# fp32 value halves, a later second rotation and another queue for B and C in a state-space stage

## The chip, the cores and the metric

The kernel runs on one core of a Trainium2 chip. The metric is the device time of one execution, in microseconds (us): 2155.58 us as the median of 3 runs of the kernel before (2154.86 to 2159.57). The profile is of one further execution, which took 2159.01 us and whose first to last instruction span 2157.2 us; 1.8 us lie around the span.

## The reference

A trunk of two layers over 256 frames of width 2048, all in fp32. Layer 0 mixes with a state-space model, layer 1 with latent attention; each is followed by a gated MLP with a causal convolution. The change touches the mixer of layer 0 alone:

```python
def s5_mixer(u, ...):                       # u: (1, 256, 2048), 128 groups of 16 channels
    # per group: a complex diagonal state of size 64, decayed by ab_re + i*ab_im at each frame
    x_re = einsum('blgp,gnp->blgn', ub, bb_re)          # and x_im
    hs_re, hs_im = scan over the frames
    y = einsum('blgn,gpn->blgp', hs_re, c_re) - einsum('blgn,gpn->blgp', hs_im, c_im) + d_skip * ub
    y = jax.nn.gelu(y)
    val, gate = jnp.split(y @ w_glu + b_glu, 2, axis=-1)   # w_glu: (2048, 4096)
    return val * sigmoid(gate)
```

The last two lines are the linear unit ("GLU"): its value half is the first 2048 columns of `w_glu`, its gate half the other 2048.

## The kernel before

**Precision.** A weight that is multiplied on the matmul engine (TensorE, PE) is loaded as fp32 into a `raw` buffer, and split there: ScalarE (ACT) writes the part `whi` that the fast one-pass type fp32r holds, VectorE (DVE) writes the rest, `wlo`. The activations are split in the same way. `mm3` (L107 to L110) makes one product of three fp32r matmuls: high by high, high by low, low by high.

**The state-space stage** (function `s5`) treats the 128 groups in 16 blocks of 8 groups. The loop over `n` runs 18 times and is a software pipeline: iteration `n` has `part_k` and `part_e` of block `n`; `part_v`, `part_r` (first rotation and the scan along the frames) and `part_h` (second rotation, of the scanned state) of block `n-1`; and `part_c` (the output) of block `n-2`. `lead_e` and `lead_f` make the operands of later blocks: products of powers of the decay with the matrices B and C (DVE, L442), two of which are added by a DMA that GpSimd (POOL) issues. `part_k` sends a matrix `K` to memory (`kd`, by ACT's queue) and reads it back in Toeplitz order (`TP`, by SyncE's queue, SP). SP also loads B and C (`bc`) and all weights.

Every fourth block a quarter of the 2048 channels is done: `part_d` applies the gelu, turns the result and writes it, split, to the activation tiles. From then on the part of the GLU that needs only this quarter's rows of `w_glu` can run. It is cut into *units*: `glu_early(f, n, b, half)` takes the rows of quarter `b`, 512 columns of the value (`half` 0) or the gate (`half` 1), 1 MB of weights, 2 splits on ACT and 2 on DVE, and 24 matmuls of 512 columns; then `glu_keep` copies or adds both results to an accumulator in SBUF. Columns 0 to 1023 of both halves are done in this way, four units to a quarter. One unit is traced at the end of an iteration where one is left. The list is worked off by a generator (`glu_steps`), and the iteration in which a generator is found to be exhausted brings no unit: quarter 0 is finished in iteration 5 and has its units in iterations 5 to 8, quarter 1 in 10 to 13, quarter 2 in 15 to 17. What is left, one unit of quarter 2 and four of quarter 3, comes first in `glu_rest`, before the 16 units of the remaining columns.

**Order.** The kernel is written for a planner which gives each engine a list in the order of the trace where the operands are there by its own costs, and lets a later instruction pass where they aren't. Each engine then works its list in order. So the matmuls of a unit lie among those of the next block. The planner also gives out the buffers of a tag: `raw` has 2, `whi` and `wlo` 3 each; the normalised input `X` occupies both `raw` buffers until `scale_x` of the last quarter.

Of the kernel before, what the change touches and what calls it, by code (L numbers as in the profile page):

```python
# [8 lines left out]
F32 = mybir.dt.float32  # L9
# [6 lines left out]
P = 128  # L16
# [28 lines left out]
def tile_trunk(ctx: ExitStack, tc: tile.TileContext, a: dict):  # L45
# [19 lines left out]
    def accb():  # L65
        return T(ps, [P, 512], F32, "acc")
# [172 lines left out]
    def glu_load(n, b, half, slots=(None, None)):  # L239
        col = half * D + n * 512  # L240
        return wunit(glu_w[b][:, :, col : col + 512], 4, 512, slots=slots)

    def glu_mm(bank, b, tb, halves):
        hk, u = halves
        for i, (wh, wl) in enumerate(u):
            for k in range(hk):
                j = i * hk + k
                mm3(bank, *acts(tb, 4 * b + j), wh[:, k, :], wl[:, k, :], b == 0 and j == 0, b == 3 and j == 3)

    def glu_early(f, n, b, half):  # L250
        hv = glu_load(n, b, half)
        banks = [accb(), accb()]
        for tb in range(NB):
            hk, u = hv
            for i, (wh, wl) in enumerate(u):
                for k in range(hk):
                    j = i * hk + k
                    mm3(banks[tb], *acts(tb, 4 * b + j), wh[:, k, :], wl[:, k, :], j == 0, j == 3)
        glu_keep(f, n, b, half, banks)
# [11 lines left out]
    def s5(f):  # L271
        with tc.tile_pool(name="s5", bufs=2) as q1, tc.tile_pool(name="dr", bufs=2, space=bass.MemoryType.DRAM) as dr:
# [7 lines left out]
            for k in range(8):  # L280
                sync.dma_start(X[k // 4][:, k % 4, :], a["xs"][k])
            gX = T(q1, [P, 512], F32, "gX", 1)
            dB = T(q1, [P, 512], F32, "dB", 1)
# [154 lines left out]
            def product(tag, bufs, sb, i):  # L438
# [4 lines left out]
                return o  # L443

            def lead_e(n):
                if n >= nb:
                    return
                if n % PB == 0:
                    zs[n // PB] = powers(n // PB)
                bc[n] = T(q1, [P, 4, NP, 16], F32, "bc", 3)  # L450
                sync.dma_start(bc[n], a["sBC"][n])
                E[n], e2 = product("e1", 3, n, 0), product("e2", 2, n, 1)
                pool.dma_start(E[n], e2, accum_op=ALU.add)
# [104 lines left out]
            def glu_steps(b):  # L558
                for n in range(2):
                    for half in range(2):  # L560
                        yield glu_early(f, n, b, half)

            def part_d(qt, yg):
                act_tiles()
                act.activation(yg, yg, AF.Gelu_apprx_tanh)
                for hh in range(2):
                    ptv = wk().rearrange("p (t m) -> p t m", t=4)
# [6 lines left out]
                    for tb in range(NB):  # L574
                        hi, lo = acts4(tb, qt, slice(0, 4))
                        src = ptv.rearrange("p t (j c) -> p t j c", j=4)[:, :, :, 16 * tb : 16 * tb + 16]
                        split(av(hi), av(lo), src)

            todo, zs, bc, E, F, fr, U, TP, ET, H = [], {}, {}, {}, {}, {}, {}, {}, {}, {}
            nb = 4 * PB  # L580

            rs = first_norm()
            lead_e(0)
            lead_f(0)
            scale_x(rs, 0)
            for n in range(nb + 2):
# [9 lines left out]
                if n < nb:  # L596
                    U[n], TP[n] = part_k(n, F[n], bc.pop(n))
                    ET[n] = part_e(E.pop(n))
                if 0 <= n - 1 < nb:
                    H[n - 1] = part_h(n - 1, R, *fr.pop(n - 1))  # L600
                if n >= 2 and m % PB == PB - 1:
                    part_d(m // PB, yg)
                    todo.append(glu_steps(m // PB))
                if n == 0:
                    lead_e(1)
                lead_f(n + 1)
                lead_e(n + 2)
                if n < 3:
                    scale_x(rs, n + 1)
                if todo and next(todo[0], True) is True:  # L610
                    todo.pop(0)
        return todo
# [588 lines left out]
```

## Time and profile before

| | |
|---|---|
| median of 3 runs | 2155.58 us (2154.86 to 2159.57) |
| profiled execution | 2159.01 us, span 2157.2 us |
| PE busy | 2057.1 us, 95% of the span |
| DVE busy | 1377.6 us, 64% |
| ACT busy | 1092.6 us, 51% |
| granted PE clock, mean of the span | 0.992 |

PE's busy time is modelled: each matmul counts to the end of its pipeline, so that the share of a stretch can be near 100% while more matmuls would fit. Instructions carry the line of the kernel; where a helper issues them (`split` is L73 on ACT and L74 on DVE, `mm3` L108 to L110, `tiled` L419), it is the helper's line, and the tiles' names tell what they are. An engine's idle time is put down to what ended it. PEld are the weight loads of PE, SPq and ACTq the instructions by which SP and ACT issue DMAs.

### The profile page before, as it was taken

The page shows a single profiled execution, that of the slowest core. Times are in us where ns is not written, and L with a number is a line of the kernel's source. Part 1 is how long each engine was busy: PE and PEld are TensorE (multiplying, and loading weights), DVE is VectorE, ACT ScalarE, POOL GpSimd, SP SyncE. Part 2 cuts the span into 40 slices and gives each one's busy share as a digit, 9 for nine tenths or more (in the row PEclk, how much of TensorE's full clock was granted, in tenths as well). Part 3 has the DMA queues.
Part 4 walks back from the last instruction along what each step waited for, and adds up shares of the span by engine and source line. Part 5 has one row for each costly group of instructions (what it writes and reads, how often), then busy time and mean ns, then how long its engine had stood idle before and what let it go on. Part 6 is the DMA issues. An engine that isn't in the chain of part 4 may idle for free.

```text
span 2157.2 us, 30703 instructions
## 1 busy us (share of the span) xinstructions
PE 2057.1 (95%) x12372; PEld 1754.2 (81%) x12372; DVE 1377.6 (64%) x1931; ACT 1092.6 (51%) x1669; POOL 32.2 (1%) x73
## 2 busy tenths in 40 slices
PE   3798998999999999999999999999999999999998
PEld 2566777888888888888878998788888888888886
DVE  8898766665466556656685665566546655665567
ACT  5565445554455445534474554655545544553444
POOL 1000000000000000000000000000000000000000
PEclk9899999999999999999999999999999999999999
DMA  5676766455555556555554334545556555555654
GB/s 148 188 197 175 236 195 190 159 195 176 196 194 187 184 195 193 180 193 194 190 193 138 123 126 152 197 156 191 180 193 197 183 187 196 189 182 189 201 184 149
DMA packets 291967, 392.15 MB, mean 182 GB/s; under 512 B 10224, under 2 KB 205424, under 8 KB 291056
## 3 DMA queue, kind: packets, MB, share of 16 engines
q1 hardware_dynamic: 287216, 377.86, 53.8%
q0 software_dynamic: 2304, 8.39, 2.2%
q10 hardware_dynamic: 2304, 3.93, 0.5%
q8 instruction: 97, 1.59, 0.3%
q14 instruction: 46, 0.38, 0.1%
HBM read 375.73 MB, written 6.03 MB: 177 GB/s over the span
## 4 chain that ended last, share of the span: by engine, by line
PE 82%; DMA 7%; DVE 6%; ACT 3%; issue 1%; SPq 0%; POOL 0%; DVEq 0%; POOLq 0%; ACTq 0%
PE wk L723 28%; PE wk L725 15%; PE acc L109 10%; PE acc L110 9%; PE acc L108 9%; DMA raw<-in_w_glu 3%; PE wk L109 2%; PE wk L110 2%; PE wk L108 2%; DVE wlo L74 1%; PE wk L419 1%; ACT whi L73 1%; DVE x L74 1%; ACT junk L135 1%; DMA kd<-K 1%
## 5 line engine op out<-in xcount | busy, mean ns | idle before, releaser
L74 DVE TENSOR_TENSOR wlo<-raw,whi 128x1024 fp32r<-128x1024 f32 (+1 forms) x636 | 755.8, 1191 | 603.5 <-ACT whi L73 597.7
L73 ACT ACTIVATE whi<-raw 128x1024 fp32r<-128x1024 f32 (+1 forms) x636 | 654.2, 1032 | 758.4 <-PE wk L723 310.5
L723 PE MATMUL wk<-act,whi 128*128 128x512 f32 x2688 | 673.6, 392 | 0.0
L723 PEld LDWEIGHTS wk<-act,whi 128*128 128x128 f32 x2688 | 483.8, 189 | 86.9
L725 PEld LDWEIGHTS wk<-act,wlo 128*128 128x128 f32 x2688 | 366.7, 190 | 26.2
L725 PE MATMUL wk<-act,wlo 128*128 128x256 f32 x2688 | 374.8, 282 | 0.0
L110 PE MATMUL acc<-whi,hl 128*128 128x512 f32 x652 | 255.9, 394 | 0.0
L109 PE MATMUL acc<-wlo,hh 128*128 128x512 f32 x652 | 255.6, 392 | 0.0
L108 PE MATMUL acc<-whi,hh 128*128 128x512 f32 x652 | 253.3, 388 | 0.0
L109 PEld LDWEIGHTS acc<-wlo,hh 128*128 128x128 f32 x652 | 122.4, 188 | 28.2
L108 PEld LDWEIGHTS acc<-whi,hh 128*128 128x128 f32 x652 | 122.4, 188 | 27.4 <-ACT hh L73 0.5
L110 PEld LDWEIGHTS acc<-whi,hl 128*128 128x128 f32 x652 | 122.6, 188 | 24.5
L108 PE MATMUL acc<-whi,act 128*128 128x512 f32 (+1 forms) x316 | 119.9, 383 | 7.2 <-ACT whi L73 4.3
L109 PE MATMUL acc<-wlo,act 128*128 128x512 f32 (+1 forms) x316 | 121.4, 385 | 2.8 <-DVE wlo L74 2.7
L110 PE MATMUL acc<-whi,act 128*128 128x512 f32 (+1 forms) x316 | 119.1, 377 | 0.4 <-DVE act L74 0.4
L782 DVE SCALAR_TENSOR_TENSOR cv<-gs,cw,cv 128x255 f32<-128x255 f32 (+1 forms) x168 | 81.0, 482 | 17.2 <-ACT cv L780 14.3
L108 PEld LDWEIGHTS acc<-whi,act 128*128 128x128 f32 x316 | 59.7, 190 | 20.1 <-ACT whi L73 5.3
L109 PEld LDWEIGHTS acc<-wlo,act 128*128 128x128 f32 x316 | 60.2, 191 | 16.8 <-DVE wlo L74 5.7
L780 ACT ACTIVATE cv<-gs,cb,cw 128x256 f32<-128x256 f32 x84 | 49.9, 594 | 45.8 <-DVE gs L731 45.8
L110 PEld LDWEIGHTS acc<-whi,act 128*128 128x128 f32 x316 | 60.1, 190 | 11.1 <-DVE act L74 0.9
L74 DVE TENSOR_TENSOR x<-raw,x 128x1024 fp32r<-128x1024 f32 x36 | 43.2, 1221 | 32.7 <-ACT x L73 32.7
L108 PE MATMUL acc<-x,act 128*128 128x512 f32 (+1 forms) x164 | 56.6, 347 | 7.1 <-DVE act L197 3.6
(277 smaller groups left out, 2243.3 us busy)
## 6 DMA issues: line engine op xcount, KB each, us to landing
raw<-in_w_gate SPq DMA_DIRECT2D x88, 1024.0 KB
raw<-in_w_up SPq DMA_DIRECT2D x88, 1024.0 KB
raw<-in_w_down SPq DMA_DIRECT2D x88, 1024.0 KB
raw<-in_w_glu SPq DMA_DIRECT2D x32, 1024.0 KB
raw<-in_w_o SPq DMA_DIRECT2D x16, 1024.0 KB
e<-e POOLq DMA_DIRECT2D x16, 512.0 KB, 6.1
TP<-kd SPq DMA_DIRECT2D x64, 128.0 KB
raw<-in_w_ukv SPq DMA_DIRECT2D x8, 1024.0 KB
```

The source lines that it names most:

```text
L73: act.activation(hi, src, AF.Copy)
L74: (eng or dve).tensor_tensor(lo, src, hi.bitcast(F32), op=ALU.subtract)
L108: pe.matmul(o, lh, rh, start=first, stop=False)
L109: pe.matmul(o, lh, rl, start=False, stop=False)
L110: pe.matmul(o, ll, rh, start=False, stop=last)
L135: act.activation(junk[:, :w], src, AF.Square, accum_out=stat)
L419: pe.matmul(o[32 * j : 32 * j + 32, g * P : (g + 1) * P], lhs(g, j), rhs(g, j), start=g == 0 and i == 0, stop=diag is None and g == NG - 1 ...
L723: pe.matmul(o, w, pair(kt), start=kt == 0, stop=False)
L725: pe.matmul(o[:, 0, :], w, pair(kt)[:, 0], start=False, stop=kt == KT - 1)
L780: act.activation(cv[:, ft, :], gv[:, ft, :], AF.Identity, scale=cw[:, 2, n : n + 1], bias=cb[:, n : n + 1])
L782: dve.scalar_tensor_tensor(cv[:, ft, sh:], gv[:, ft, : S - sh], cw[:, 2 - sh, n : n + 1], cv[:, ft, sh:], op0=ALU.mult, op1=ALU.add,)
```

## The change

1. **Value halves in fp32.** For quarters 0 to 2, the units of the value half multiply plain fp32 tiles: `part_d` keeps an unsplit copy `plain` of the quarter (4 more copies on ACT), the weights are loaded, as two DMAs of 512 KB, into one buffer each of `whi` and `wlo` instead of `raw`, they aren't split, and a unit has 8 fp32 matmuls in place of 24 fp32r ones. Gate halves, and all of quarter 3, stay as they were.
2. **Units in three steps.** A unit is now traced in three pieces (load and first 128 frames; last 128 frames; `glu_keep`). The first lies between `part_e` and `part_h`, so that the matmul of the second rotation is traced behind it, the others at the end of the iteration. `advance` goes on to the next quarter's generator when one is exhausted: an iteration has one unit from iteration 5 to 17, and quarters 0, 1 and 2 are done in iterations 5 to 16. `part_d` stands before `part_h` now.
3. **B and C.** `bc` is loaded three blocks ahead by ACT's queue, right behind `part_k`, instead of two blocks ahead by SP's (the first three still by SP).
4. `scale_x` of the last quarter is done in iteration 1 instead of 2, and `gX` shares the buffer of `yg`.

```diff
+    plain = {}
+
     def glu_early(f, n, b, half):
-        hv = glu_load(n, b, half)
         banks = [accb(), accb()]
+        if half == 0 and b in plain:
+            raws = [T(env["wp"], [P, 2, 512], F32, t, env["wb"]) for t in ("whi", "wlo")]
+            for i, raw in enumerate(raws):
+                sync.dma_start(raw, glu_w[b][:, 2 * i : 2 * i + 2, n * 512 : (n + 1) * 512])
+        else:
+            hk, u = glu_load(n, b, half)
         for tb in range(NB):
-            hk, u = hv
-            for i, (wh, wl) in enumerate(u):
-                ...
+            if half == 0 and b in plain:
+                for j in range(4):
+                    pe.matmul(
+                        banks[tb], plain[b][:, j, tb * P : (tb + 1) * P], raws[j // 2][:, j % 2, :],
+                        start=j == 0, stop=j == 3,
+                    )
+            else:
+                ...
+            yield
         glu_keep(f, n, b, half, banks)
...
-            gX = T(q1, [P, 512], F32, "gX", 1)
+            gX = T(q1, [P, 512], F32, "yg", 1)
...
+            def fetch(n, eng):
+                if n < nb:
+                    bc[n] = T(q1, [P, 4, NP, 16], F32, "bc", 3)
+                    eng.dma_start(bc[n], a["sBC"][n])
+
             def lead_e(n):
...
-                bc[n] = T(q1, [P, 4, NP, 16], F32, "bc", 3)
-                sync.dma_start(bc[n], a["sBC"][n])
...
-                        yield glu_early(f, n, b, half)
+                        yield from glu_early(f, n, b, half)
+                        yield
...
                 act.activation(yg, yg, AF.Gelu_apprx_tanh)
+                if qt < 3:
+                    plain[qt] = T(q1, [P, 4, S], F32, "plain", 1)
...
                         split(av(hi), av(lo), src)
+                        if qt < 3:
+                            act.activation(av(plain[qt][:, :, tb * P : (tb + 1) * P]), src, AF.Copy)
...
+            def advance():
+                while todo and next(todo[0], True) is True:
+                    todo.pop(0)
+
             rs = first_norm()
+            for n in range(3):
+                fetch(n, sync)
...
                     U[n], TP[n] = part_k(n, F[n], bc.pop(n))
+                    fetch(n + 3, act)
                     ET[n] = part_e(E.pop(n))
-                if 0 <= n - 1 < nb:
-                    H[n - 1] = part_h(n - 1, R, *fr.pop(n - 1))
                 if n >= 2 and m % PB == PB - 1:
                     part_d(m // PB, yg)
                     todo.append(glu_steps(m // PB))
+                advance()
+                if 0 <= n - 1 < nb:
+                    H[n - 1] = part_h(n - 1, R, *fr.pop(n - 1))
                 if n == 0:
                     lead_e(1)
                 lead_f(n + 1)
                 lead_e(n + 2)
-                if n < 3:
+                if n < 2:
                     scale_x(rs, n + 1)
-                if todo and next(todo[0], True) is True:
-                    todo.pop(0)
+                if n == 1:
+                    scale_x(rs, 3)
+                advance()
+                advance()
```

More of the change, by code (lines that the diff above doesn't have):

```diff
@@ L248, in glu_mm @@
                 mm3(bank, *acts(tb, 4 * b + j), wh[:, k, :], wl[:, k, :], b == 0 and j == 0, b == 3 and j == 3)
+    plain = {}
     def glu_early(f, n, b, half):
-        hv = glu_load(n, b, half)
         banks = [accb(), accb()]
-        for tb in range(NB):
-            hk, u = hv
-            for i, (wh, wl) in enumerate(u):
-                for k in range(hk):
-                    j = i * hk + k
-                    mm3(banks[tb], *acts(tb, 4 * b + j), wh[:, k, :], wl[:, k, :], j == 0, j == 3)
+        if half == 0 and b in plain:
[4 more added lines that the diff above has]
+            hk, u = glu_load(n, b, half)
+        for tb in range(NB):
+            if half == 0 and b in plain:
[5 more added lines that the diff above has]
+            else:
+                for i, (wh, wl) in enumerate(u):
+                    for k in range(hk):
+                        j = i * hk + k
+                        mm3(banks[tb], *acts(tb, 4 * b + j), wh[:, k, :], wl[:, k, :], j == 0, j == 3)
+            yield
         glu_keep(f, n, b, half, banks)
```

## The prediction

> **What bounds the kernel now.** I read the page first. PE is busy for 95% of the span, so outside the stage that is changed the matmuls set the time, and nothing there is touched. The question is what one stage is worth.
>
> ```profile
> span 2157.2 us, 30703 instructions
> PE 2057.1 (95%) x12372; PEld 1754.2 (81%) x12372; DVE 1377.6 (64%) x1931; ACT 1092.6 (51%) x1669; POOL 32.2 (1%) x73
> ```
>
> Next, the timeline of PE for the places of the loop. Below stand `part_k` of block 5 (iteration 5), the first matmul of the first GLU unit, and `part_k` of block 15.
>
> ```profile
> 82.78 0.67 PE L419 MATMUL wk<-f,bc 128*32 128x128 f32 x16
> ...
> 90.19 0.51 PE L108 MATMUL acc<-whi,act 128*128 128x512 f32 x1
> ...
> 215.96 1.08 PE L419 MATMUL wk<-f,bc 128*32 128x128 f32 x32
> ```
>
> I call 80 to 216 us the stretch: ten iterations, 5 to 14. Then the busy time by stretches (each engine: busy us and instructions; then PE clock, DMA share, GB/s):
>
> ```profile
> 100.00:120.00 20.00, 19.57 (x276) 15.55 (x274) 20.00 (x37) 12.46 (x28) 1.06 (x4) 1.00 0.65 193
> 80.00:216.00 136.00, 118.20 (x1498) 91.07 (x1493) 121.78 (x195) 79.17 (x153) 8.99 (x14) 0.95 0.67 180
> 216.00:240.00 24.00, 23.84 (x246) 19.54 (x246) 15.39 (x25) 13.35 (x21) 0.00 (x0) 1.00 0.62 193
> 240.00:300.00 60.00, 54.39 (x228) 41.64 (x227) 42.09 (x55) 27.41 (x35) 0.00 (x0) 1.00 0.78 237
> ```
>
> The third figure of a row is PE, the fifth DVE. In the stretch DVE is busy for 121.8 of 136 us (89.5%), and from 100 to 120 without a pause: DVE is the first limit there. PE has 17.8 us without a matmul. From 216 on PE takes over. DVE's groups in the stretch show what it does:
>
> ```profile
> L442 DVE TENSOR_TENSOR f<-zs,bc 128x1024 f32<-128x1024 f32 x20 | 24.2, 1217 | 1.3 <-PE wk L419 1.3
> L442 DVE TENSOR_TENSOR e<-zs,bc 128x1024 f32<-128x1024 f32 x20 | 24.1, 1218 | 0.0
> L74 DVE TENSOR_TENSOR wlo<-raw,whi 128x1024 fp32r<-128x1024 f32 x19 | 22.7, 1219 | 0.0
> L268 DVE TENSOR_TENSOR f<-acc,f 128x512 f32<-128x512 f32 x8 | 5.5, 682 | 8.8 <-PE acc L110 8.8
> ```
>
> The 19 weight splits are 22.7 us of it. PE's GLU matmuls in the same stretch are 66 + 68 + 66 = 200, or 8.3 units of 24:
>
> ```profile
> L109 PE MATMUL acc<-wlo,act 128*128 128x512 f32 x66 | 28.1, 426 | 0.0
> L108 PE MATMUL acc<-whi,act 128*128 128x512 f32 x68 | 28.0, 426 | 7.2 <-ACT whi L73 4.3 <-ACT act L73 2.8
> L110 PE MATMUL acc<-whi,act 128*128 128x512 f32 x66 | 27.0, 409 | 0.4 <-DVE act L74 0.4
> ```
>
> **Part 1, the fp32 halves.** First PE's price. Below are 22 `mm3` matmuls without a pause, then fp32 matmuls of attention, 256 and 128 columns.
>
> ```profile
> 186.06 0.50 PE L109 MATMUL acc<-wlo,act 128*128 128x512 f32 x1
> ...
> 190.94 0.39 PE L110 MATMUL acc<-whi,act 128*128 128x512 f32 x1
> ```
> ```profile
> L968 PE MATMUL acc<-krO,rpo 128*128 128x256 f32 x16 | 4.8, 379 | 0.0
> ...
> L968 PE MATMUL acc<-krO,rpo 128*128 128x128 f32 x16 | 3.1, 275 | 0.0
> ```
>
> The first pair gives (190.94 - 186.06) / 21 = 0.232 us each, 5.6 us a unit. For fp32, 128 columns more cost 379 - 275 = 104 ns, and the code's 8 products per shape and tile name appear as 16 records: two passes. A pass of 512 columns is then about 4 x 0.104 = 0.42, with the 0.02 that a 512-column fp32r matmul has over 0.21 some 0.43 us; 8 products x 2 x 0.43 = 6.9 us. A fp32 unit costs PE **1.3 us more**. No 512-column fp32 matmul is in the trace: at least 6.7 (104 ns scaled), at most 7.4 (four thirds of 5.6). With five such units in the stretch: +6.5 us; the sixth comes after it.
>
> DVE: in the stretch only the gate units are split, 5 done and one ahead, 11 or 12 splits in place of 19: 8 x 1.22 = 9.8 us less. ACT loses 8 x 1.06 and gains, at three ends of quarters, 4 copies of the shape that it writes for `act`, 12 x 0.68 = 8.1 us:
>
> ```profile
> L73 ACT ACTIVATE whi<-raw 128x1024 fp32r<-128x1024 f32 x16 | 17.0, 1060 | 27.2 <-PE acc L110 11.9 <-DMA raw<-in_w_glu 10.3 <-DVE e L442 4.9
> ...
> L73 ACT ACTIVATE act<-wk 128x256 fp32r<-128x256 f32 x12 | 7.0, 675 | 0.5 <-PE wk L569 0.5
> ```
>
> ACT stays at some 79 of 136 us and isn't the limit. But the first of these rows shows ACT standing 10.3 us for weights, with the copies `K` and `vs` queued behind; for half of the units that wait goes. What is late next is PE itself, if the 512 KB loads are late. I price this at nothing: the freed `whi` and `wlo` buffers let the load go out at the end of the last value unit, two iterations ahead. Without that cover it would be what ACT waits today, 10.3 us over 8.3 units, so 1.2 us a unit and 7.4 for six: the sum below would be -0.1.
>
> **Part 2, order and pace.** By iteration 14, ten units are traced instead of 8.3, by iteration 16 twelve. Up to 240 us the kernel before has done 11.2: the GLU matmuls from 216 to 240 (groups below) are 69, or 2.9 units more.
>
> ```profile
> L109 PE MATMUL acc<-wlo,act 128*128 128x512 f32 x24 | 9.7, 403 | 0.0
> L108 PE MATMUL acc<-whi,act 128*128 128x512 f32 x22 | 9.0, 410 | 0.0
> L110 PE MATMUL acc<-whi,act 128*128 128x512 f32 x23 | 9.0, 391 | 0.0
> ```
>  So 0.8 of a unit leaves the part behind the stage. There, 228 matmuls took 60 us, 6.3 us per unit of 24: **-5.0 us**, if the stage itself gets no longer.
>
> The stretch then has 1.7 units more: on PE 1.7 x 5.6 + 6.5 = 16 us, in all 134.2 by the view's count; on DVE 1.7 x 2 x 0.68 = 2.3 for the sums, in all 121.8 - 9.8 + 2.3 = 114.3. How long will it be? If DVE keeps its share of 89.5%, 114.3 / 0.895 = 128 us, -8. If PE sets it, at the share of 100 to 120 (19.57 of 20), 134.2 / 0.979 = 137, +1. Neither has a reason to win, as the two engines come out nearly level; I take the middle, 132.5: **-3.5 us**.
>
> The close, 216 to 240, loses its cover: now 2.9 units lie around the last block's chain, then two. These rows are its last part:
>
> ```profile
> 233.00 1.28 ACT L565 ACT_TABLE_LOAD   x1
> ...
> 234.30 1.06 ACT L565 ACTIVATE yg<-yg 128x1024 f32<-128x1024 f32 x1
> ...
> 238.65 2.04 ACT L73 ACTIVATE whi<-raw 128x1024 fp32r<-128x1024 f32 x2
> ```
>
> PE work falls by 0.9 x 5.6 = 5.0 us and rises by 1.3: at best -3.7. At worst the 5.65 us from 233.00 to 238.65 lie bare where one unit less fills them: +3. I take **+1**, nearer the chain, since the gelu and the splits must follow the last block in any order.
>
> The second rotation behind the first half of a unit: PE waits little for it now (last row; the waits of the stretch, in us, times, longest).
>
> ```profile
> ACT whi L73 <- DMA raw<-in_w_glu: 10.3, 4, 3.8
> ...
> DVE w L518 <- PE wk L516: 3.6, 5, 2.2
> PE wk L531 <- DVE R L526: 3.5, 5, 1.3
> ```
>
> 3.5 us in the stretch could go; I count them within the range of the stretch, not again.
>
> **Parts 3 and 4: nothing.** SP's waits from 47 to 216 us, ACT's issue of one DMA, and the DVE part of `scale_x`, two of them for a quarter:
>
> ```profile
> SPq L488 <- DMA kd<-K: 78.2, 14, 8.4
> SPq L451 <- PE wk L426: 23.5, 9, 4.6
> ```
> ```profile
> 104.73 0.33 ACTq L484 DMA_DIRECT2D kd<-K  x1
> ```
> ```profile
> L358 DVE TENSOR_TENSOR raw<-raw,gX 128x512 f32<-128x512 f32 x8 | 5.5, 685 | 0.0
> ```
>
> SP stands 23.5 us for the buffers of `bc`, but 78.2 for `kd` right after, and the latter covers it: `TP` would be no sooner. On ACT each fetch takes 0.33 us, 13 in all, 4.3 us, behind `K`, which waits for the same matmuls; the queue behind is `ET` and `vs`. If ACT were the limit, that would be +4.3. `scale_x` moves 1.4 us of DVE forward by one iteration, ahead of the first unit; nothing is behind it that is late.
>
> **Sum.** -3.5 + 1 - 5.0 = -7.5. The profiled execution of 2159.0 would be 2151.5; the median of the runs stands 3.4 below that execution, so 2155.6 - 7.5 = **2148.1 us**. Extremes of the terms: -8 - 3.7 - 5.0 = -16.7 and +1 + 3 - 5.0 = -1.0.
>
> One thing is left out of it: the clock, 0.95 in the stretch. After two waits it was about half:
>
> ```profile
> 168.13 0.73 PE L108 MATMUL acc<-whi,act 128*128 128x512 f32 x1 [3.21 <-ACT whi L73]
> ...
> 201.70 0.63 PE L110 MATMUL acc<-whi,act 128*128 128x512 f32 x1
> ...
> 205.11 0.63 PE L109 MATMUL acc<-wlo,act 128*128 128x512 f32 x1
> ```
>
> The last two are 8 matmuls apart: 0.426 us each instead of 0.232, 1.6 us lost; as much again at most near 168. The Trainium skill, "TensorE: Matmul & The Clock Gate", in "Part 1: The HAM clock gate", says that an idle window of about 3.4 us halves the clock. By that rule, fewer waits would bring another -3 us (2145); the wait of 3.21 fits it roughly. I leave it within the range.
>
> **Rivals.** *A, my forecast*, 0.45: 2143 to 2152.
>
> *B, DVE was all of it*, 0.18: the stretch follows DVE, PE's small gaps fill; -16.7, 2138.9. For it: DVE at 20.00 of 20. Against: PE would need 134.2 us by the view's count within 128, which takes overlap of the modelled ends.
>
> *C, PE is the new limit, or the planner lets the units lag*, 0.20: -1.0, 2154.6. For it: 134.2 us of PE work in a stretch of 136. Against: ends overlap more when matmuls are dense. If the extra unit isn't done before the close, the -5.0 falls away and the sum is -2.5, 2153. This is also the change not doing what it says.
>
> *D, slower*, 0.17: one mechanism, `part_h` behind half a unit. The half is 2.8 us (fp32r) or 3.5 (fp32); `part_h`'s multiplies on DVE and all products queued behind them wait for it, then `part_c` one iteration on. If 1.5 us of it shows in each of 12 iterations, +18 against -7.5: 2166. It decides from 7.5 / 12 = 0.6 us an iteration. For it: DVE now waits 3.6 us for the first rotation and 8.8 for GLU results, so PE's order does reach DVE. Against: the planner lets a ready rotation pass a unit whose weights aren't there.
>
> **Numbers.** A change of 0.2% (4.3 us) is about what a measurement tells from none. Faster by more: B, and A but for its upper edge, 0.60; within: C, that edge and D's lower end, 0.25; slower: 0.15. The range, 2137 to 2160, goes from below B to part of D and leaves out D's centre.
>
> **What would show it.** Right: 12 fewer `wlo` splits, 48 fp32 products (96 records) of 512 columns with starts 0.43 us apart, DVE's stretch busy near 114 us, iteration 15's `part_k` near 212, and the first unit of quarter 3 near 237 with twelve units before it. Wrong: fp32 passes well over 0.46 us; waits of PE for the new weight loads; DVE's `w` L534 waiting for L531 by more than 0.6 us an iteration; fewer than twelve units at the close.

## The result and the profile after

The changed kernel took 2174.82 us (median of 4 runs, 2172.26 to 2175.70) against 2157.51 us for the kernel before on the same chip: a ratio of **1.0078, with a 95% interval from 1.0065 to 1.0090**. It is slower by 17 us, where I had forecast 2148.1 us, faster by 7.5 than the 2155.6 known then. The profiled execution's span went from 2157.2 to 2172.8 us.

From the page of the changed kernel, the span and the busy times of the engines:

```profile
span 2172.8 us, 30607 instructions
PE 2070.7 (95%) x12324; PEld 1752.1 (81%) x12324; DVE 1364.9 (63%) x1919; ACT 1088.5 (50%) x1669; POOL 32.3 (1%) x73
```

DVE lost 12.7 us of work, PE gained 13.6. The shares look as before, so the page does not tell where 16 us came from. The timeline of PE does. Its rows give the start, the length, and the instructions; here are `part_k` of blocks 5 and 15, and the first matmul of the norm's turn, ahead of the first MLP:

```profile
81.19 0.73 PE L433 MATMUL wk<-f,bc 128*32 128x128 f32 x17
...
233.46 1.08 PE L433 MATMUL wk<-f,bc 128*32 128x128 f32 x32
...
382.07 2.16 PE L189 MATMUL acc<-xh,x 128*128 128x128 f32 x17
```

Block 15 began at 216.0 before and begins at 233.5 now: 17.5 us of loss lie in the ten iterations that the prediction called the stretch. The norm's turn begins at 382.1 instead of 368.7, so the part between gives back only 4.1, and some 2 us more come behind it.

The windows of the changed kernel (length, then busy us and instructions of PE, PEld, DVE, ACT, POOL, then clock, DMA share, GB/s): the stretch, the 20 us in which DVE had no pause before, the close, and what follows up to the norm's turn.

```profile
80.00:233.50 153.50, 132.32 (x1474) 91.07 (x1476) 115.32 (x186) 81.06 (x159) 9.01 (x14) 0.93 0.64 171
100.00:120.00 20.00, 18.29 (x247) 13.49 (x245) 16.21 (x30) 10.73 (x25) 1.92 (x4) 1.00 0.66 173
...
233.50:253.30 19.80, 19.34 (x209) 13.33 (x208) 11.43 (x22) 6.38 (x11) 0.00 (x0) 1.00 0.31 94
253.30:382.10 128.80, 118.18 (x489) 91.78 (x489) 79.02 (x103) 64.76 (x83) 1.15 (x3) 0.97 0.72 213
```

The busy times are near what the prediction said: PE 132.3 (134.2 forecast), DVE 115.3 (114.3 forecast). For PE this is luck in part, since its busy time holds records at half clock that were not forecast (below). The **length** is not as forecast: 153.5 us instead of 132.5. DVE is busy for 75% of it and no longer without a pause between 100 and 120. PE stands for 153.5 - 132.3 = 21.2 us; before, it stood for 17.8. Work was added and the sum of the pauses did not shrink: 134.2 + 17.8 = 152.0 would have been nearly right. But they are not the same pauses. These rows are the longest groups of PE's waits (total us, times, longest), from 80 to 216 us before, then from 80 to 233.5 in the changed kernel:

```profile
PE acc L108 <- ACT whi L73: 4.3, 2, 3.2
PE wk L515 <- ACT vs L506: 4.1, 2, 2.4
```
```profile
PE wk L433 <- DVE H L557: 7.3, 3, 4.7
PE wk L589 <- ACT yg L583: 5.4, 2, 3.7
PE wk L433 <- DVE w L551: 4.1, 3, 1.8
```

Before, PE waited for split weights, for `vs`, and 3.5 us for `R`. The wait for split weights is gone and the other two have shrunk to 0.8 together; in their place PE waits for the rotated state `H`, for the gelu `yg`, for the product `w` of the second rotation, and for `plain`. I have no reason to give for the two sums being so close.

What the added work is, from the groups of PE in that stretch (instructions, busy us, mean ns, then the idle time before them):

```profile
L263 PE MATMUL acc<-whi,plain 128*128 128x512 f32 x40 | 22.0, 679 | 2.6 <-ACT plain L599 2.6
L263 PE MATMUL acc<-wlo,plain 128*128 128x512 f32 x40 | 20.7, 644 | 0.0
L108 PE MATMUL acc<-whi,act 128*128 128x512 f32 x40 | 17.0, 426 | 0.0
L110 PE MATMUL acc<-whi,act 128*128 128x512 f32 x40 | 15.7, 393 | 0.0
L109 PE MATMUL acc<-wlo,act 128*128 128x512 f32 x40 | 15.7, 391 | 0.0
```

Five fp32 units (80 records) and five split ones, ten in all, as forecast. PE waits for the copies `plain`, never for the fp32 weights.

Most of the pauses lie at the ends of the quarters; the waits for `H` lie between them. PE's timeline at the second quarter's end:

```profile
147.67 1.09 PE L589 MATMUL wk<-cst,yg 128*128 128x128 f32 x8 [1.71 <-ACT yg L583]
...
151.57 0.43 PE L433 MATMUL wk<-TP,U 128*32 128x128 f32 x8 [1.33 <-DVE w L551]
153.93 3.78 PE L263 MATMUL acc<-whi,plain 128*128 128x512 f32 x4 [1.93 <-ACT plain L599]
157.51 3.14 PE L263 MATMUL acc<-wlo,plain 128*128 128x512 f32 x4
160.48 1.88 PE L263 MATMUL acc<-whi,plain 128*128 128x512 f32 x4
162.20 1.88 PE L263 MATMUL acc<-wlo,plain 128*128 128x512 f32 x4
164.01 0.64 PE L433 MATMUL wk<-f,H 128*32 128x128 f32 x16
```

PE waits for the gelu (1.71), then for the second rotation's product `w` (1.33), then for the last copies (1.93). Then the fp32 unit stands in one block, from 153.93 to 164.01, and the next block's output (`wk<-f,H`) comes behind it. Its first four records start (157.51 - 153.93) / 4 = 0.90 us apart, its last (162.20 - 160.48) / 4 = **0.43 us**, which is the price I had estimated: the unit runs at half clock at first. ACT's timeline shows why the copies are late:

```profile
145.26 1.28 ACT L583 ACT_TABLE_LOAD   x1
146.56 1.06 ACT L583 ACTIVATE yg<-yg 128x1024 f32<-128x1024 f32 x1
...
149.29 1.12 ACT L73 ACTIVATE act<-wk 128x256 fp32r<-128x256 f32 x2
150.43 1.28 ACT L419 ACT_TABLE_LOAD   x1
151.73 0.72 ACT L419 ACTIVATE co<-co,cst 128x512 f32<-128x512 f32 x1
152.35 0.61 ACT L599 ACTIVATE plain<-wk 128x256 f32<-128x256 f32 x1
152.76 0.67 ACT L73 ACTIVATE act<-wk 128x256 fp32r<-128x256 f32 x1
153.21 0.67 ACT L599 ACTIVATE plain<-wk 128x256 f32<-128x256 f32 x1
```

The first copies for the split unit (`act`) are made from 149.29 on; the first `plain` is made 3.06 us later, behind a table load and the cosine of the next powers. In the kernel that makes both copies but multiplies split ones (`copies_only`, below), the unit at the same place starts without a wait behind the first `act`, and the output stands only 6.7 us behind its start:

```profile
147.17 1.37 PE L589 MATMUL wk<-cst,yg 128*128 128x128 f32 x8 [1.71 <-ACT yg L583]
...
150.62 0.78 PE L108 MATMUL acc<-whi,act 128*128 128x512 f32 x1
...
157.04 0.39 PE L110 MATMUL acc<-whi,act 128*128 128x512 f32 x1
157.36 0.64 PE L433 MATMUL wk<-f,H 128*32 128x128 f32 x16
```

The longest single wait of the stretch is none of these. It is one for `H`, on PE, and it has its cause on DVE, whose row stands below it:

```profile
202.61 1.08 PE L433 MATMUL wk<-f,H 128*32 128x128 f32 x16 [4.75 <-DVE H L557]
```
```profile
198.94 2.36 DVE L456 TENSOR_TENSOR e<-zs,bc 128x1024 f32<-128x1024 f32 x2 [6.35 <-DMA bc<-in_sBC]
```

DVE stands 6.35 us until a load of B and C lands. Two products for a later block are ahead of the rest of the second rotation in its list, so `H` is late, PE stands 4.75 us, and its next 16 records take 1.08 us instead of 0.64. Such waits for `bc` come to 10.5 us in three places here; the kernel before has none.

### The profile page after: what moved, and what is told of

Its sections match the earlier page's. It is cut to its first block, busy times and chain, and to the rows that moved or that the text cites. A ratio compares the mean times of both kernels' runs of the same rounds, so it can differ in the third digit from the quotient of the medians.

```text
span 2172.8 us, 30607 instructions
## 1 busy us (share of the span) xinstructions
PE 2070.7 (95%) x12324; PEld 1752.1 (81%) x12324; DVE 1364.9 (63%) x1919; ACT 1088.5 (50%) x1669; POOL 32.3 (1%) x73
## 4 chain that ended last, share of the span: by engine, by line
PE 83%; DVE 6%; DMA 6%; ACT 3%; issue 1%; POOL 0%; SPq 0%; DVEq 0%; ACTq 0%; POOLq 0%
PE wk L755 28%; PE wk L757 15%; PE acc L110 9%; PE acc L109 9%; PE acc L108 9%; DMA raw<-in_w_glu 2%; PE acc L263 2%; PE wk L109 2%; PE wk L110 2%; PE wk L108 2%; DVE wlo L74 1%; PE wk L433 1%; ACT whi L73 1%; DVE x L74 1%; DVE e L456 1%; DMA raw<-in_w_ukv 1%
## 5 line engine op out<-in xcount | busy, mean ns | idle before, releaser
L74 DVE TENSOR_TENSOR wlo<-raw,whi 128x1024 fp32r<-128x1024 f32 (+1 forms) x624 | 741.5, 1191 | 609.3 <-ACT whi L73 600.2
L73 ACT ACTIVATE whi<-raw 128x1024 fp32r<-128x1024 f32 (+1 forms) x624 | 641.5, 1031 | 755.9 <-PE wk L755 295.2
L108 PE MATMUL acc<-whi,act 128*128 128x512 f32 (+1 forms) x268 | 102.0, 382 | 2.0 <-ACT whi L73 1.3
L109 PE MATMUL acc<-wlo,act 128*128 128x512 f32 (+1 forms) x268 | 100.5, 375 | 0.1
L110 PE MATMUL acc<-whi,act 128*128 128x512 f32 (+1 forms) x268 | 99.9, 373 | 0.0
L108 PEld LDWEIGHTS acc<-whi,act 128*128 128x128 f32 x268 | 51.0, 190 | 12.1 <-ACT whi L73 2.6
L109 PEld LDWEIGHTS acc<-wlo,act 128*128 128x128 f32 x268 | 51.0, 190 | 9.8 <-DVE wlo L74 1.2
L110 PEld LDWEIGHTS acc<-whi,act 128*128 128x128 f32 x268 | 50.9, 190 | 9.0 <-DVE act L74 0.2
```

The costliest lines, as they stand in the source:

```text
L73: act.activation(hi, src, AF.Copy)
L74: (eng or dve).tensor_tensor(lo, src, hi.bitcast(F32), op=ALU.subtract)
L108: pe.matmul(o, lh, rh, start=first, stop=False)
L109: pe.matmul(o, lh, rl, start=False, stop=False)
L110: pe.matmul(o, ll, rh, start=False, stop=last)
```

## The experiments

All ratios are to the kernel before, with 95% intervals. For the stretch of each I give, from the windows of its trace between `part_k` of blocks 5 and 15, the length, PE's busy time, and the difference, called pauses: 133.2 = 115.5 + 17.7 for the kernel before, 152.3 = 131.5 + 20.8 for the changed one. "Before" and "after" name the kernel that an edit starts from, and "..." marks lines left out.

**Parts undone one by one.** `values_split`, after without part 1 (the value units are split again):

```diff
-                if qt < 3:
-                    plain[qt] = T(q1, [P, 4, S], F32, "plain", 1)
...
-                        if qt < 3:
-                            act.activation(av(plain[qt]...), src, AF.Copy)
```

> Changed kernel with all values split as before: no fp32 copies, 24 fp32r matmuls in each unit, weights through the raw buffers; order, three steps and queue as changed. Theory F: the loss goes, 2155 to 2160. Theory E: the rotation still stands behind the gelu at the three quarter ends; at most the difference of the units' PE time goes, 6 x 1.3 = 8 us, and DVE has 12 splits of 1.22 us more: 2166 to 2174. Theory Q: 2173.

Measured: 2156.53 us, 0.9995 [0.9986, 1.0005]. Stretch 141.7 = 123.0 + 18.7. Without the fp32 halves the whole loss is gone; parts 2 to 4 together are worth nothing. They lengthen the stretch by 8.5 us, 7.5 of it work, and the part behind the stage is shorter for it.

`rot_first`, after with the second rotation traced ahead of the output step and the unit's first piece again, in all iterations:

```diff
+                if 0 <= n - 1 < nb:
+                    H[n - 1] = part_h(n - 1, R, *fr.pop(n - 1))
                 if n >= 2 and m % PB == PB - 1:
                     part_d(m // PB, yg)
                     todo.append(glu_steps(m // PB))
                 advance()
-                if 0 <= n - 1 < nb:
-                    H[n - 1] = part_h(n - 1, R, *fr.pop(n - 1))
```

> Changed kernel, but the second rotation is traced before the quarter's output step and before the first piece of the unit, as in the kernel before; everything else as changed. Theory E (quarter ends): in the changed kernel the matmul of the rotation at 89.81 us stands behind the output step's transposes at 88.17, which wait 3.69 us for the gelu; the last block's output waits for it, PE idles, its clock halves, and the unit that follows takes 8.8 us instead of 6.9. Three quarters have this; the end of the stage is 20 us later than before. With the rotation first nearly all of it should go: 2156 to 2161. Theory F (fp32 is the cost): the six fp32 units and the waits on their results are the loss whatever the order; 2170 or more. Theory Q (queue of B and C): no change, 2173 or more.

Measured: 2168.80 us, 1.0053 [1.0038, 1.0068]. Stretch 148.9 = 127.8 + 21.1. This lies between the ranges of theories E and F. It is some 5 us at most, a third of the loss; the pauses are as long as in the changed kernel, though other waits make them up (`H` 0.3 instead of 7.3, `vs` 7.1 instead of 0.5). PE's busy time is 3.7 lower, though the number of its instructions (1469) is the same: the clock is 0.95 instead of 0.93.

`bc_sp`, after with B and C loaded by SP two blocks ahead:

```diff
+                fetch(n, sync)          # in lead_e
...
-                    fetch(n + 3, act)
```

> Changed kernel, but B and C are loaded two blocks ahead by SyncE's queue as before. DVE waited 10.5 us in three places for them in the changed kernel, and never in the one before. Theory Q: these waits are on the path; 2164 or less. Theories E and F: DVE has slack of more than that behind the quarter ends; 2172 to 2176.

Measured: 2168.76 us, 1.0055 [1.0038, 1.0071]. Stretch 147.4 = 125.4 + 22.0. DVE's waits for `bc` are still 11.2 us, so the queue is not what makes these loads late, and this run does not say what their lateness costs.

`rot_bc`, both edits together:

> Changed kernel with the rotation first (as in the run of that name) and B and C by SyncE's queue, both at once; the fp32 values and the three steps stay. Alone each took some 5 us off. If they are two losses (order; late B and C): 2157 to 2163. If both only move the same thing, PE's clock in the fp32 unit behind a quarter's end (10.2 us for the second such unit in the changed kernel, 7.2 in either run): 2165 to 2170.

Measured: 2169.85 us, 1.0042 [1.0028, 1.0056]. Stretch 151.3 = 131.5 + 19.8. The two don't add, so at least one of the two 5 us isn't a price of its own. The planner makes another order with each edit, and I take this as the first sign of how much that alone does.

**Parts done alone.** `before_plain`, before with parts 1 and 4:

```diff
     def glu_early(f, n, b, half):
...
+        if half == 0 and b in plain:
+            raws = [T(env["wp"], [P, 2, 512], F32, t, env["wb"]) for t in ("whi", "wlo")]
...
+                    pe.matmul(banks[tb], plain[b]..., raws[j // 2]..., start=j == 0, stop=j == 3)
```

> Kernel before with the fp32 value halves alone (and the earlier scaling of the last quarter that makes room for the copy): units in one piece at the end of an iteration, rotation before the output step, pace and queue as before. Theory F: 2165 or more. Theory E: the quarter ends are as before, so the fp32 units cost at most their PE time (8 us) and give back up to 14.6 us of DVE: 2150 to 2160.

Measured: 2160.37 us, 1.0015 [1.0006, 1.0025]. Stretch 136.3 = 117.8 + 18.6. At the old pace the fp32 halves cost 2 to 3 us; at the new one 18.

`before_bc`, before with part 3:

```diff
+            def fetch(n, eng): ...
-                sync.dma_start(bc[n], a["sBC"][n])
...
+                    fetch(n + 3, act)
```

> Kernel before with B and C three blocks ahead by ACT's queue, nothing else. The prediction priced this at nothing (2156 to 2160). The rival: DVE waited 10 to 13 us for B and C in all runs with the change's parts, and never in the kernel before, so loading them by ACT makes them late: 2163 or more.

Measured: 2160.42 us, 1.0001 [0.9985, 1.0016]. Part 3 alone is worth nothing; DVE's waits for `bc` are one of 3.5 us here.

**Which engine sets the pace.** `half_products`, after with the fp32 products of two of the four row blocks left out (so half of the value's sum over quarters 0 to 2 is missing in these units), 20.7 us of PE at 0.43 us a record:

```diff
-                for j in range(4):
+                for j in range(2):
...
-                        start=j == 0, stop=j == 3,
+                        start=j == 0, stop=j == 1,
```

> Changed kernel with half of the fp32 products left out (2 of the 4 row blocks of each value unit; the output lacks them; all loads and copies stay). This takes 6 x 3.45 = 21 us of matmul time off PE and nothing else. If PE's time is the limit of the stage, most of it shows: 2152 to 2160. If the loss is the wait at the quarter ends or for DMAs: 2166 to 2174.

Measured: 2143.35 us, 0.9926 [0.9905, 0.9947]. That is 31 us less than after, for 20.7 us of work, and more than either theory allowed. Stretch 133.1 = 117.0 + 16.1. In the profiled executions the norm's turn begins 25.5 us sooner (356.5 instead of 382.1). Nearly 8 us more come behind it, where the edit changes nothing: from the norm's turn to the end of the span the kernels here take 1783 to 1792 us without a reason that I know. So some 25 of the 31 us belong to the stage.

`dve_twice`, before with the 12 `wlo` splits of those value units made twice, 12 x 1.22 = 14.6 us more on DVE:

```diff
-        (eng or dve).tensor_tensor(lo, src, hi.bitcast(F32), op=ALU.subtract)
+        for _ in range(env.get("times", 1)):
+            (eng or dve).tensor_tensor(lo, src, hi.bitcast(F32), op=ALU.subtract)
...
+        env["times"] = 2 if half == 0 and b < 3 else 1
         hv = glu_load(n, b, half)
```

> Kernel before with the 12 DVE splits of the value units of quarters 0 to 2 done twice: 14.6 us more on DVE, the rest as before. My prediction's step: DVE is the first limit of the stretch, so most of it shows, 2167 to 2173 against 2158. The rival (PE's list sets the pace and DVE only runs ahead of it): less than 4 us, 2156 to 2162.

Measured: 2166.09 us, 1.0031 [1.0019, 1.0043]: +6.7 us. This is just short of what my step expected and more than the rival did, so work added to DVE does show in part.

`no_wlo`, before with the same 14.6 us taken away; `whi` takes the place of `wlo`, so the weights' low part is left out and the high part counts twice, at the same work for PE:

```diff
-        (eng or dve).tensor_tensor(lo, src, hi.bitcast(F32), op=ALU.subtract)
+        if not env.get("hi"):
+            (eng or dve).tensor_tensor(lo, src, hi.bitcast(F32), op=ALU.subtract)
...
-                lo = T(wp, [P, hk, cols], F32R, "wlo", nb)
+                lo = hi if env.get("hi") else T(wp, [P, hk, cols], F32R, "wlo", nb)
```

> Kernel before, but the value units of quarters 0 to 2 are not split on DVE: their 24 fp32r matmuls take whi in place of wlo, so the low parts of these weights are left out of the result. It takes the change's 12 splits, 14.6 us, off DVE at the same PE time. If DVE is the first limit as predicted: 2144 to 2150. If DVE and PE each carry about half, as the doubled splits say (+6.7 for 14.6): 2150 to 2154. If DVE only has slack to give: 2156 to 2160.

Measured: 2155.15 us, 0.9985 [0.9973, 0.9997]: -3.3 us. The windows of this kernel are its stretch, here from 80 us on as in the prediction, and the 20 us in which DVE had been full:

```profile
80.00:213.20 133.20, 115.40 (x1500) 91.41 (x1501) 110.14 (x181) 81.42 (x156) 9.02 (x14) 0.95 0.69 185
100.00:120.00 20.00, 19.46 (x236) 15.79 (x230) 17.74 (x32) 14.02 (x29) 1.92 (x4) 1.00 0.77 201
```

DVE has 11.6 us less to do than the 121.8 of before, and the stretch is 2.8 us shorter. A microsecond taken off DVE returns about a quarter of itself. So **DVE's work, full as it was between 100 and 120, was not what set the length of the stretch**. That does not put DVE out of the chain: in this kernel PE stands 12.8 us, in seven places, until DVE gives `R`, the scanned state (3.5 us before). DVE can be late with one result while its total work is no limit.

`keep_late`, after with the third step of a unit (the sums on DVE) traced an iteration later, against the waits of DVE for the fp32 results:

```diff
+                advance()
                 if n >= 2 and m % PB == PB - 1:
...
                 advance()
-                advance()
```

> Changed kernel, but the third step of a unit (the add or copy of its result) is traced one iteration later, behind the next block's part_e, instead of at once. In the changed kernel DVE stood 19.2 us in six places for the results of fp32 units, with the products for later blocks queued behind. If these waits are on the path: 2162 to 2168. If DVE has the time to wait and the fp32 price is PE's alone: 2171 to 2176.

Measured: 2173.71 us, 1.0068 [1.0046, 1.0091]. This one tells little: DVE's wait in front of the sums is still there. The rows of the waits of DVE from 80 to 260 us, first after, then `keep_late` (total us, times, longest):

```profile
DVE f L282 <- PE acc L263: 19.2, 6, 5.4
```
```profile
DVE f L282 <- PE acc L263: 19.7, 6, 4.7
```

Whether these 19 us cost anything was not settled by it.

**What is it at the quarters' ends.** `copies_only`, after with split value units, and the `plain` copies still made but not read:

```diff
-        if half == 0 and b in plain:
+        if False:
...
-            if half == 0 and b in plain:
+            if False:
```

> Changed kernel with split values as in the run of that name (2156.5), but the fp32 copies of the quarters are still made on ACT and not used. The prediction priced them at nothing: 2154 to 2159. If ACT at the quarter ends is on the path, 3 x 4 x 0.68 = 8 us at most: 2160 to 2165.

Measured: 2150.45 us, 0.9966 [0.9953, 0.9979]. Stretch 135.4 = 121.5 + 13.9. No cost of the copies as work of ACT shows. The kernel is even 6 us faster than `values_split`, which differs only in not making them, and I know of no way in which making the copies would save time. The traces show where most of it lies: DVE's waits for `bc` are 6.5 us instead of 12.2 and PE's for `H` 4.2 instead of 9.2. I read these 6 us as what another order by the planner is worth, and take no difference of that size between two single kernels as a price.

`copies_first`, after with the `plain` copies of a quarter made ahead of its split ones:

```diff
-                        split(av(hi), av(lo), src)
                         if qt < 3:
                             act.activation(av(plain[qt]...), src, AF.Copy)
+                        else:
+                            split(av(hi), av(lo), src)
+                    if qt < 3:
+                        for tb in range(NB): ...
+                            split(av(hi), av(lo), src)
```

> Changed kernel with the fp32 copies of a quarter made before its splits on ACT, so that the first fp32 unit can start 2 to 3 us sooner. If the wait for the copies, and the half clock that follows it, is most of the loss: 2162 to 2168. If the unit's own length before the last output is: 2171 to 2175.

Measured: 2166.54 us, 1.0041 [1.0027, 1.0056]. Stretch 145.2 = 126.8 + 18.4.

`gate_first`, after with the halves swapped, so that a quarter's first unit is a split one and the fp32 unit comes in mid-quarter:

```diff
-                    for half in range(2):
+                    for half in (1, 0):
```

> Changed kernel with the order of the halves swapped in each pair of units: gate (split) first, value (fp32) second, so that no fp32 unit stands at the end of a quarter. The same work on every engine. Theory K (the loss is the fp32 unit at the quarter's end: late copies, half clock, one block before the last output): 2154 to 2162. Theory L (fp32 matmul time costs its price anywhere): 2170 or more.

Measured: 2168.49 us, 1.0048 [1.0033, 1.0063]. Stretch 149.4 = 131.1 + 18.4. The summary of the fp32 products by tile gives the shortest, median and longest in ns, first for after, then for `gate_first`:

```profile
L263 PE MATMUL acc<-whi,plain x48: 592/592/1223, 94.4 to 240.6; 128*128 128x512 f32 x48
```
```profile
L263 PE MATMUL acc<-whi,plain x48: 592/592/595, 104.4 to 246.6; 128*128 128x512 f32 x48
```

Away from the quarter's end every fp32 product runs at full clock. The half clock did not go, however: in the stretch PE's busy time and clock are 131.1 us and 0.93, as in after, so it now falls on other matmuls. In `copies_first` they are 126.8 us and 0.96, and the first fp32 unit takes 7.1 us. The edits take off 6 and 8 us, hardly more than the planner's 6, and `gate_first` lies between the ranges of its two theories. That the place of the fp32 unit, ahead of the copies it needs, is part of the price is therefore likely, by both edits and the trace, but not shown by the times alone.

`rot_first_q`, after with the rotation ahead of the output step at the three quarter ends only, and `gate_first_rotq`, the same with the gate first:

```diff
+                ends = n >= 2 and m % PB == PB - 1
+                if ends:
+                    if 0 <= n - 1 < nb:
+                        H[n - 1] = part_h(n - 1, R, *fr.pop(n - 1))
...
-                if 0 <= n - 1 < nb:
+                if 0 <= n - 1 < nb and not ends:
                     H[n - 1] = part_h(n - 1, R, *fr.pop(n - 1))
```

> The changed kernel with the rotation before the output step in the three iterations that end a quarter only; fp32 value first as in the change. Theory K: as with the rotation first everywhere (2168.8), 2165 to 2170, since the fp32 unit still stands before the last output. If the waits for the gelu and the rotated state alone are the loss: 2155 to 2162.

> The changed kernel with gate first, and in the iterations that end a quarter the rotation before the output step. With split values the latter gave 5 us (2156.5 to 2151.2). If both act on their own: 2150 to 2157. If they repeat each other: as gate first alone within 3 us.

Measured: `rot_first_q` took 2174.45 us, 1.0079 [1.0061, 1.0097], no gain at all and outside both ranges, with a stretch of 155.5 = 131.3 + 24.2; `gate_first_rotq`, with the gate first, took 2160.54 us, 1.0015 [1.0003, 1.0027], stretch 142.1 = 127.1 + 15.0. The same edit is worth 0 in the one and 8 us in the other. Why it fails where the fp32 unit comes first is open; the unit in one block behind the late copies is there in both after and `rot_first_q`.

`split_rotq`, the same edit and split value units:

> Changed kernel with split values as in the run of that name, and in the iterations that end a quarter the rotation is traced before the output step. In that run PE waited 8.2 us for the gelu and 9.2 for the rotated state, three times each. If these waits are on the path: 2146 to 2152. If the unit's matmuls fill what is gained and PE's time is the limit: 2153 to 2158.

Measured: 2151.16 us, **0.9960 [0.9943, 0.9976]**, faster than both kernels. Against `gate_first_rotq` it has no fp32 and the value first: 9.4 us less, where six units of fp32 cost PE 6 x 1.3 = 8 us. Its stretch is 134.3 = 120.8 + 13.6: at the pace of the changed kernel PE has 5.3 us more work than before, and 4.1 us of the pauses did close.

**PE's time, or fp32 itself?** `pe_more`, `split_rotq` with six more one-pass products in each of the six value units, 8.3 us in all; some high products are counted twice, so what is computed is changed:

```diff
+                        if half == 0 and b < 3 and j < 3:
+                            pe.matmul(banks[tb], acts(tb, 4 * b + j)[0], wh[:, k, :], start=False, stop=False)
```

> Split value units and the rotation ahead of the output step at the three quarter ends (the kernel that took 2151.2 us), with six more one-pass matmuls, about 0.23 us each at full clock, in each of the six value units of quarters 0 to 2: their high products are counted twice, so what is computed is changed. It puts 6 x 1.4 = 8.3 us of TensorE time back where the fp32 halves had put it, with no fp32. If the price of the fp32 halves is TensorE's time alone, the time rises to about 2159 to 2162 us. If it lies in fp32 itself, it stays near 2151 us.

Measured: 2167.54 us (2163.14 to 2175.29), 1.0057 [1.0034, 1.0080]. The windows of the stretch of `split_rotq`, then of `pe_more`:

```profile
80.90:215.20 134.30, 120.75 (x1505) 96.17 (x1504) 125.11 (x195) 84.85 (x155) 8.99 (x14) 0.96 0.74 194
```
```profile
81.80:230.50 148.70, 129.14 (x1535) 103.35 (x1534) 125.41 (x194) 85.13 (x155) 8.99 (x14) 0.95 0.66 174
```

The time is above the 2159 to 2162 that PE's time alone was to give. In the stretch PE is busy for 8.4 us more: 30 more products, 7.0 us at 0.23, and the rest is a lower clock. DVE has the same work, and the stretch is 14.4 us longer: the pauses grow from 13.6 to 19.6. No fp32 was needed for that. The longest group of PE's waits in `pe_more` is for `H`, the state that the second rotation gives, behind which the output is queued:

```profile
PE wk L435 <- DVE H L559: 10.3, 5, 3.3
```

The same row in `split_rotq`:

```profile
PE wk L433 <- DVE H L557: 1.1, 1, 1.1
```

This is the same chain as at 202 us of the changed kernel. DVE waits 10.4 us for `bc`, in four places, where it waits 1.6 in `split_rotq`, and three of the five waits for `H` come right behind. So part of what `pe_more` loses beyond its added work is late loads of B and C. Why they come later here, no run shows.

`split_rotq_bc`, `split_rotq` with B and C by SP as before:

> Split value units, the rotation ahead of the output step at the three quarter ends, and B and C loaded by SyncE's queue two iterations ahead, as before. If ScalarE's queue costs something once the values are split, the time falls below 2148 us; if the place of these two loads is worth nothing, it stays at 2148 to 2154 us.

Measured: 2147.73 us, **0.9952 [0.9937, 0.9966]**, the fastest of the kernels that leave nothing out. Stretch 132.9 = 120.0 + 13.0. The interval overlaps that of `split_rotq`; the queue's worth is not told apart from nothing. In this kernel DVE never waits for `bc`, and PE never for `H`.

The stretch of some of these in one table (us):

| kernel | length | PE busy | pauses | DVE busy | ratio |
|---|---|---|---|---|---|
| before | 133.2 | 115.5 | 17.7 | 119.3 | 1 |
| `dve_twice` | 141.3 | 116.9 | 24.4 | 125.5 | 1.0031 |
| `half_products` | 133.1 | 117.0 | 16.1 | 112.7 | 0.9926 |
| `split_rotq` | 134.3 | 120.8 | 13.6 | 125.1 | 0.9960 |
| `values_split` | 141.7 | 123.0 | 18.7 | 124.5 | 0.9995 |
| `gate_first_rotq` | 142.1 | 127.1 | 15.0 | 114.6 | 1.0015 |
| `pe_more` | 148.7 | 129.1 | 19.6 | 125.4 | 1.0057 |
| after | 152.3 | 131.5 | 20.8 | 114.1 | 1.0078 |

PE's work nearly puts the lengths in order, DVE's does not: rows with some 125 us of it are 134, 141, 142 and 149 us long. PE's busy time is not work alone, since a record at half clock counts for longer (the fp32 records of after last 0.59 to 1.22 us). The shortest pauses of all kernels are the 13.0 us of `split_rotq_bc`.

## Why the prediction was wrong, point by point

**The step that failed is the length of the stretch**, -3.5 us forecast, +17.5 measured. I had taken the middle between 128 (DVE keeps its share) and 137 (PE at the share of 100 to 120). Both ends were wrong in the same way: each let the 17.8 us in which PE stood close, because I took them for time lost to DVE, "the first limit there". `no_wlo` shows that they were not lost to DVE's amount of work: with DVE lighter by 11.6 us the stretch gained 2.8. In the changed kernel they came out at 21.2 us, and no longer the same ones: PE now stands where results come one after another, for the gelu, `w` and `plain` at a quarter's end, and for `H` where B and C land late. That some length must be left for such waits is what the sums missed; how much depends on the order, 13 to 24 us in the kernels here, and in `split_rotq` 4.1 of the 17.7 did close. That DVE was busy for 20.00 of 20 us proved that it had a supply of work, not that anybody waited for it.

From `values_split` and after the 19.1 us by which the stretch grew can be read in two steps: parts 2 to 4, 7.5 us of work and 1.0 of pauses; the fp32 halves, 8.5 us of work and 2.1 of pauses. Of these 8.5, five units at 1.3 are 6.5, and I read the rest as more half clock than in `values_split`, whose clock is 0.95. The steps' sizes carry the planner's 6 us of uncertainty. The first is not a price of the pace: `split_rotq` has the same pace, and its stretch is 134.3, only 1.1 longer than before.

**The fp32 price** of +1.3 us a unit was right where the clock was full: 0.43 us a record. In after, the first and third fp32 units took 8.8 and 10.1 us instead of the 7.1 of the fifth, which stands at a quarter's end too but ran at full clock; so 4.7 us more. What was missed is that little came back for it: the 12 splits that went were worth some 3 us in `no_wlo`.

**Plain copies priced at nothing, since ACT "isn't the limit".** As work that holds: `copies_only` makes them and is fast. As a dependency it does not: the quarter's first unit waits for them at the end of ACT's queue (2.6 us in three waits), and `copies_first` and `gate_first` take 8 and 6 us off, little more than another order can. ACT's busy share could not show that; the order on ACT behind the gelu could.

**Weight loads at nothing**: right, no wait of PE in front of L263 is for a DMA. **Parts 3 and 4 at nothing**: right for the queue of part 3 (`before_bc`, 1.0001; `split_rotq_bc` not told apart); part 4 was only run with part 1. What the prediction did not ask is whether `bc` would be there in time when DVE came for it. In the changed kernel it was not, and one of PE's waits, 4.75 us, hangs on that. It is not the queue: `bc_sp` has these waits too, and so has `before_plain` (13.1 us of DVE), with almost no loss.

**The unit less behind the stage, -5.0**: right in kind. From the stage's end to the norm's turn it took 135.7 us before (233.0 to 368.7) and 128.8 after, so -6.9. **The close, +1**: the time from block 15 to the end of the stage went from 17.0 to 19.8, so +2.8. With +17.5 the three make the +13.4 of the norm's turn.

**The clock.** I had left 3 us of gain within the range for fewer waits. It went the other way, 0.95 to 0.93 in the stretch. The Trainium skill, "TensorE: Matmul & The Clock Gate", "Part 1: The HAM clock gate", puts the drop after at least one idle window of about 3.4 us. Two of the drops here agree: PE's records take about 1.7 times as long behind the wait of 3.69 us at 88.17 (1.84 us for eight, against 1.09) and behind the 4.75 us at 202.61. The third does not: PE ran at half clock from 153.93 on after pauses of 1.71, 1.33 and 1.93 us, none of them as long as that, with 0.43 us of matmuls between the last two; so short waits close together were enough, and the longest wait alone does not tell.

**The rivals.** *A* and *B* fell with DVE. *C* named the right engine with the wrong sum: its 137 us is PE's work with next to no pauses. *D* had the sign, and PE's waits for `H` and `w` (11.4 us together, 0.5 before) are of its kind. But its own sign, DVE's `w` waiting for the second rotation on PE, does not show, its 1.5 us per iteration would make 18 us, and the rotation put back gave about 5 in all iterations, nothing at the quarter ends alone, and is not added to by the other queue. What carries the loss is that PE's added work was not hidden: without the fp32 halves it is gone, and with half of their products left out too. They cost 8 us at full clock; the rest is half clock and waits in the order that the planner made, and no run tells these two apart.

**What remains open**: why the rotation's place helps with a split unit behind it and not with an fp32 one; whether DVE's 19 us of waits for the fp32 results cost anything; what the late loads of B and C cost, since no kernel here loads them earlier with the rest unchanged; and how much of each step is the planner's order.

## What to carry to other kernels

An engine that is busy for 100% of a stretch is its limit only if the others wait for it: look whether their idle time is put down to it before giving its work to another engine. When work is added to an engine that stands now and then, take its length with all pauses kept as one bound, and let them close only where a row shows what fills them: here the changed kernel closed none, and the best order some 5 of 18 us. And where a consumer moves to a new copy of its operand, read how late that copy comes on its engine, not how busy the engine is.

## What was not expected of the hardware

One microsecond of PE work in this stage came out as more than one: 8.4 us more of busy time went with a stretch 14.4 us longer (`pe_more`), and 20.7 us of products left out brought the norm's turn 25.5 us forward (`half_products`). What goes beyond one is 5 to 6 us in each, no more than another order can make. One on DVE is worth a quarter to a half (-3.3 and +6.7 us for 14.6). And an fp32 record of 512 columns, which at full clock starts 0.43 us after the one before it, took up to 0.90 us behind waits that were each shorter than 2 us.
